# One fused decoder kernel on Trainium2: attention issued by upper and lower heads in turn

## The chip, the cores and the metric

The kernel runs on one core of a Trainium2 chip. The metric is the device time of one execution in microseconds. The engines are TensorE (PE; its weight loads are PEld), VectorE (DVE), ScalarE (ACT), GpSimd (POOL) and SyncE (SP), which here issues DMAs. Each has its own instruction stream, takes it in order, and waits on semaphores where it needs another engine's result.

## What is computed

256 tokens of width 1024 in fp32 go through: an even layer (sliding-window attention with 8 heads beside a state space mixer), a feed-forward net, an odd layer (stick-breaking attention with 16 heads), a second feed-forward net, a third one, the mix stage (spatial gating beside dilated-window attention with 8 heads), cross attention, a last feed-forward net and a norm. The heads are 64 wide in the three attentions that matter here. The parts of the reference that the change touches, cut:

```python
# even layer
scores = einsum('bnqhgd,bnkhd->bnhgqk', qb, kb) * d ** -0.5     # banded mask
m = maximum(scores.max(-1), sink); p = exp(scores - m)
o = einsum(..., p / (p.sum(-1) + exp(sink - m)), vb)
out = y * sigmoid(y @ w_glu + b_glu)                            # y: the SSM's gelu'd output
mixed = concatenate([o_attn, o_ssm], -1) @ even_w_out
# odd layer: A[t,s] = beta_ts * prod_{s<j<t}(1 - beta_tj), s < t
z = einsum('bhqd,bhkd->bhqk', q, k) * scale
log_keep = where(mask, log_sigmoid(-z), 0)
log_survive = cumsum(log_keep, reverse=True) - log_keep
w = where(mask, exp(log_sigmoid(z) + log_survive), 0);  o = einsum(w, v)
# mix stage
y_a = chunked_spatial_gating(z_sgu);  y_b = dilated attention(q, k, v)
y = concatenate([rmsnorm(y_a), rmsnorm(y_b)], -1);  x = x + y @ w_out
```

## The kernel before

Activations stay in SBUF as two token tiles of 128. Weights stream in by DMA in tiles of 128x1024 (`raw`); ACT casts each to its upper part (L293, `whi`) and DVE subtracts for the lower part (L295, `wlo`). Where full precision is wanted, a product is three TensorE products (L320, L321, L322): upper by upper, lower by upper, upper by lower. These are the "GEMM products" below.

A list scheduler sets the order on every engine from the order in which the program is written, so what the text issues in a row may be interleaved with other work. The coarse order of the three stages is set by strings: `EVEN`, `ODD` and `MIX`, whose two-letter items name pieces (`10` is step 0 of the attention of token tile 1; `g0` in `MIX` is the gating of tile 0; `K0` to `K3` are projections of the memory for the later cross attention, work that depends on nothing in the stage).

PSUM has eight banks of 128 partitions by 512 fp32 in three pools: `mm` (2), `tr` (2) and `acc` (4).

A head is 64 wide, so two heads lie one above the other in the 128 partitions: the lower half (0 to 63) and the upper half (64 to 127). A score product has 64 rows of contraction and uses half the rows of the array. A value product has 64 output rows and uses half the columns.

`attention()` serves the even stage (t0 and t1) and the mix stage. Its `step(g)` takes `per` heads of one half: one score bank (`mm`), the mask added by a product with the identity (L587), the scores (L591), maximum, exponential (L605), normalisation (L612), four transposes (L401), one copy out of PSUM (L619), and the value products (L625) into the bank `po`. There are 2 steps for t0 and 4 for t1.

In the odd stage `scores(b, half)` takes four heads of one half and three blocks (lower keys by lower queries, lower by upper, upper by upper), each in its own `acc` bank: mask (L1188), scores (L1191), DVE minimum (L1194), ACT Exp (L1195). `weights` follows with Ln (L1206), DVE maximum (L1207), the cast `sph` and the remainder `spl` (L1210, L1211), products with triangular and all-one matrices (L1218) and Exp (L1221, `w0` and `w1`). `values` (L1234, L1236) writes two `tr` banks. `before(q)` writes the outputs of the state space mixer (L1094). `ssm_gate` transposes them (L401 out of `s0`), splits them (DVE copy L1114, ACT cast L1115, DVE L1116) and multiplies by the gate's weights.

In the mix stage `normed` (L1309 to L1314) is run for both halves of the output, `oa` (gating) and `ob` (attention), each for two token tiles: ACT Square, POOL addition, PE column sums (L419), DVE mean (L423), POOL power (L424), DVE diagonal (L426), PE broadcast (L429), ACT copy (L431), DVE scaling (L1314), ACT cast (L396), DVE remainder (L397). Then `w_out` takes `oa` first.

Of the kernel before, what the change touches and what calls it, by code (L numbers as in the profile page):

```python
# [16 lines left out]
P = 128  # L17
# [220 lines left out]
class Kernel:  # L238
# [331 lines left out]
    def attention(self, pool, t, qt, kt, kblock, v, vcol, bias, nsink):  # L570
# [12 lines left out]
        def step(g):  # L583
            sc = self.ps("mm")
            scv = sc.rearrange("p (h k) -> p h k", h=per)
            for m, bt in enumerate(bias):
                nc.tensor.matmul(sc, self.ident_r, bt, start=(m == 0), stop=False)  # L587
            for i in range(per):
                half, qb = divmod(g * per + i, 4)
                r = slice(half * 64, half * 64 + 64)  # L590
                nc.tensor.matmul(scv[:, i, :], qt[r, qb, t * P:(t + 1) * P],  # L591
                                 kt[r, kblock(qb), 0:keys], start=False, stop=(i == per - 1))
            hs = slice(g * per, (g + 1) * per)
# [8 lines left out]
            pr = self.t(pool, [P, per, keys], "prob", bufs=4)  # L602
            for i in range(per):
                h = g * per + i
                nc.scalar.activation(pr[:, i, :], scv[:, i, :], AF.Exp, bias=mneg[:, h:h + 1],  # L605
                                     scale=SCALE, accum_out=den[:, h:h + 1])
# [11 lines left out]
            pt = self.t(pool, [P, 4, P], "prob", bufs=4)  # L618
            nc.scalar.copy(pt, tp.rearrange("p (c n) -> p c n", c=4))  # L619
            for i in range(per):  # L620
                half, qb = divmod(g * per + i, 4)
                r = slice(half * 64, half * 64 + 64)
                h = 2 * qb + half
                for b in range(nk):
                    nc.tensor.matmul(po[r, qb * P:(qb + 1) * P], v[b][:, vcol(h):vcol(h) + 64],  # L625
                                     pt[:, i * nk + b, :], start=(b == 0), stop=(b == nk - 1))

        return [lambda g=g: step(g) for g in range(8 // per)], po.rearrange("p (b n) -> p b n", b=4)


# [430 lines left out]
    def ssm_out(self, ep, uu, S):  # L1061
# [26 lines left out]
        def before(q):  # L1088
            hs = S["hs"]
            for gl in range(4 * q, 4 * q + 4):  # L1090
                bank, cols = at(gl)
                r = (gl % 2) * 64
                for ri in range(2):
                    nc.tensor.matmul(yb[bank][r:r + 64, cols], hs[ri][:, gl, :], gts[q][:, ri, gl % 4],  # L1094
                                     start=False, stop=(ri == 1), skip_group_check=True)
# [7 lines left out]
    def ssm_gate(self, ep, gy):  # L1103
# [16 lines left out]
        for pr in range(2):  # L1120
# [6 lines left out]
            for b in range(2):  # L1127
                o = 2 * pr + b
                sg = self.t(ep, [P, 256], "prob", bufs=4)
                nc.scalar.activation(sg, ps[:, b * 256:(b + 1) * 256], AF.Sigmoid,  # L1130
                                     bias=self.prm[:, PR_BGLU + o:PR_BGLU + o + 1])
                y = self.t(ep, [P, 256], "prob", bufs=4)
# [24 lines left out]
    def odd(self):  # L1157
# [18 lines left out]
        blocks = ((lo_, lo_), (lo_, hi_), (hi_, hi_))  # L1176

        parts = {}

        def scores(b, half):  # L1180

            r = slice(half * 64, half * 64 + 64)
            zs, raw = [], []
            for n, (s, t) in enumerate(blocks):
                z = self.ps("acc")
                zv = z.rearrange("p (h t) -> p h t", h=4)
                if n != 1:
                    nc.tensor.matmul(zv, self.ident_r, stk.unsqueeze(1).to_broadcast([P, 4, P]),  # L1188
                                     start=True, stop=False)
                for i in range(4):  # L1190
                    nc.tensor.matmul(zv[:, i, :], kt[r, b * 4 + i, s], qt[r, b * 4 + i, t],  # L1191
                                     start=(n == 1 and i == 0), stop=(i == 3))
                sp = self.t(op, [P, 512], "sp", bufs=3)
                nc.vector.tensor_scalar(sp, z, 40.0, None, ALU.min)  # L1194
                e = nc.scalar.activation(sp, sp, AF.Exp).ins  # L1195
                zs.append(z)
                raw.append(sp)
            parts[b, half] = zs, raw, e

        def weights(b, half):  # L1200
            zs, raw, e = parts[b, half]
            sps = []
            for z, sp in zip(zs, raw):

                with self.tc.issue_after(e):
                    nc.scalar.activation(sp, sp, AF.Ln, bias=1.0)  # L1206
                nc.vector.tensor_tensor(sp, sp, z, ALU.max)  # L1207
                sh = self.t(op, [P, 512], "sph", F32R, bufs=3)
                sl = self.t(op, [P, 512], "spl", F32R, bufs=3)
                nc.scalar.copy(sh, sp)  # L1210
                nc.vector.tensor_tensor(sl, sp, sh.bitcast(F32), ALU.subtract)  # L1211
                sps.append((sh, sl))
            w0 = self.t(op, [P, 4, 256], "w0", bufs=2)
            w1 = self.t(op, [P, 4, P], "w1", bufs=2)
# [344 lines left out]
```

## Time and profile before

| | us |
|---|---|
| time, median of 3 runs | 1247.03 |
| lowest and highest | 1245.78, 1249.15 |
| profiled execution, own time | 1243.83 |
| its span in the trace | 1242.1 |
| PE busy | 1211.7 (98%) |
| DVE busy | 868.8 (70%) |
| ACT busy | 676.6 (54%) |
| POOL busy | 211.2 (17%) |

The span is what the trace covers; the own time is 1.73 us longer. Approximate stages in the span: even layer 0 to 165, feed-forward to 343, odd layer 343 to 475, feed-forward nets to 840, mix 840 to 975, cross attention to 1030, the last feed-forward net and norm to the end. A matmul's busy time includes its passage through the array, so consecutive ones overlap in the records; the distance between two starts is their pace.

### The profile page before, as it was taken

To read this page: it belongs to the slowest core of one execution; us is meant where nothing else is said; L and a number is where in the kernel's file an instruction comes from. 1 tells how busy PE (TensorE), PEld (TensorE's weight loads), DVE (VectorE), ACT (ScalarE), POOL (GpSimd) and SP (SyncE) were. 2 spreads that over 40 slices of the span, in tenths; PEclk is the share of its full clock that TensorE was granted. 3 is DMA by queue.
4 is the path that set the end of the run, shared out by engine and by line. 5 is a ranking of instruction groups with operands and counts; after the bars stand their busy time and mean duration, and the time that the engine had idled before them with its cause. 6 is when DMAs were issued, how large, how long until landed. Compare 5 with 4: busy or idle time off the path is not lost.

```text
span 1242.1 us, 19044 instructions
## 1 busy us (share of the span) xinstructions
PE 1211.7 (98%) x7686; PEld 1072.7 (86%) x7686; DVE 868.8 (70%) x1191; ACT 676.6 (54%) x1052; POOL 211.2 (17%) x177
## 2 busy tenths in 40 slices
PE   6889999999999999999999999999999999999997
PEld 6777998888899879888888888888889999888886
DVE  8978588777665647877766867766866656777752
ACT  6543566565446755655545655545664545655542
POOL 7665021110010002101001110002201101111000
PEclk9978999999999999999999999999999999999998
DMA  6541355555553325455654545646633434555551
GB/s 208 172 158 53 139 172 194 180 201 203 180 197 110 131 68 204 170 187 186 216 191 174 196 177 198 204 174 212 209 131 103 155 118 139 190 183 201 204 200 38
DMA packets 36776, 208.86 MB, mean 168 GB/s; under 512 B 3920, under 2 KB 9808, under 8 KB 12752
## 3 DMA queue, kind: packets, MB, share of 16 engines
q1 hardware_dynamic: 35824, 205.48, 47.7%
q0 software_dynamic: 576, 1.64, 0.5%
q8 instruction: 60, 0.98, 0.3%
q10 hardware_dynamic: 288, 0.52, 0.1%
q14 instruction: 28, 0.23, 0.1%
HBM read 205.57 MB, written 2.06 MB: 167 GB/s over the span
## 4 chain that ended last, share of the span: by engine, by line
PE 92%; DVE 5%; DMA 1%; issue 1%; ACT 1%; POOL 0%; DVEq 0%; ACTq 0%
PE acc L367 26%; PE acc L366 13%; PE mm L367 13%; PE mm L366 7%; PE mm L320 4%; PE mm L322 4%; PE mm L321 4%; PE acc L322 4%; PE acc L321 4%; PE acc L320 4%; PE mm L591 1%; PE tr L401 1%; PE acc L1191 1%; DVE wlo L295 1%; PE acc L625 1%; DVE a L454 1%
## 5 line engine op out<-in xcount | busy, mean ns | idle before, releaser
L295 DVE TENSOR_TENSOR wlo<-raw,whi 128x1024 fp32r<-128x1024 f32 (+1 forms) x378 | 472.0, 1251 | 225.1 <-ACT whi L293 223.6
L293 ACT CAST whi<-raw 128x1024 fp32r<-128x1024 f32 (+1 forms) x378 | 392.4, 1043 | 280.8 <-DMA raw<-in_wts 111.2
L367 PE MATMUL acc<-h,whi 128*128 128x512 f32 x704 | 247.8, 397 | 0.0
L367 PE MATMUL mm<-a,whi 128*128 128x512 f32 x704 | 247.0, 392 | 0.0
L367 PE MATMUL acc<-a,whi 128*128 128x512 f32 x704 | 246.0, 392 | 0.0
L366 PE MATMUL acc<-h,wlo 128*128 128x256 f32 x704 | 196.9, 281 | 0.0
L366 PE MATMUL mm<-a,wlo 128*128 128x256 f32 x704 | 196.6, 281 | 0.0
L366 PE MATMUL acc<-a,wlo 128*128 128x256 f32 x704 | 196.3, 280 | 0.0
L367 PEld LDWEIGHTS acc<-h,whi 128*128 128x128 f32 x704 | 131.9, 188 | 32.0
L367 PEld LDWEIGHTS mm<-a,whi 128*128 128x128 f32 x704 | 131.5, 187 | 28.5
L367 PEld LDWEIGHTS acc<-a,whi 128*128 128x128 f32 x704 | 130.9, 187 | 28.2
L366 PEld LDWEIGHTS acc<-a,wlo 128*128 128x128 f32 x704 | 133.0, 189 | 1.0
L366 PEld LDWEIGHTS acc<-h,wlo 128*128 128x128 f32 x704 | 132.9, 189 | 0.3
L366 PEld LDWEIGHTS mm<-a,wlo 128*128 128x128 f32 x704 | 132.6, 189 | 0.2
L546 POOL TENSOR_TENSOR sg<-sg,rb 128x512 f32<-128x512 f32 x44 | 58.2, 1326 | 388.8 <-ACT sg L545 379.2
L463 POOL TENSOR_TENSOR ssq<-ssq,sq 128x512 f32<-128x512 f32 x26 | 39.7, 1528 | 416.7 <-ACT sq L461 253.2
L320 PE MATMUL mm<-a,whi 128*128 128x256 f32 x224 | 66.4, 298 | 6.7 <-ACT whi L293 6.7
L321 PE MATMUL acc<-a,whi 128*128 128x256 f32 x240 | 67.4, 284 | 0.0
L322 PE MATMUL acc<-a,wlo 128*128 128x256 f32 x240 | 67.1, 285 | 0.0
L322 PE MATMUL mm<-a,wlo 128*128 128x256 f32 x224 | 66.1, 296 | 0.8 <-DVE wlo L295 0.7
L320 PE MATMUL acc<-a,whi 128*128 128x256 f32 x240 | 66.0, 286 | 0.0
L321 PE MATMUL mm<-a,whi 128*128 128x256 f32 x224 | 65.8, 295 | 0.0
(371 smaller groups left out, 1951.5 us busy)
## 6 DMA issues: line engine op xcount, KB each, us to landing
raw<-in_wts SPq DMA_DIRECT2D x187, 1024.0 KB, 4.9
raw<-in_mem SPq DMA_DIRECT2D x4, 512.0 KB, 5.6
eb<-lag SPq DMA_DIRECT2D x4, 512.0 KB, 4.8
x<-in_x SPq DMA_DIRECT2D x4, 256.0 KB, 5.3
raw<-in_wts SPq DMA_DIRECT2D x4, 256.0 KB, 5.6
sprm<-in_prm SPq DMA_DIRECT2D x1, 512.0 KB, 9.1
ud<-s SPq DMA_DIRECT2D x1, 512.0 KB, 2.6
uu<-ud SPq DMA_DIRECT2D x8, 64.0 KB, 5.3
```

Of the source, the lines that this page charges most:

```text
L293: nc.scalar.copy(hi[:, c:c + n], src)
L295: nc.vector.tensor_tensor(lo[:, c:c + n], src, hi[:, c:c + n].bitcast(F32), ALU.subtract)
L320: mm(out, a[0], b[0], start=start, stop=False, skip_group_check=True)
L321: mm(out, a[0], b[1], start=False, stop=False, skip_group_check=True)
L322: mm(out, a[1], b[0], start=False, stop=stop, skip_group_check=True)
L366: mm(out[:, 0, :], w[1], x[:, 0], start=first, stop=False, skip_group_check=True)
L367: mm(out, w[0], x, start=False, stop=last, skip_group_check=True)
L401: self.nc.tensor.transpose(out, in_, self.ident[:k, :k])
L454: lo = nc.vector.scalar_tensor_tensor(lo, x[:, b, :], g, hi.bitcast(F32), ALU.mult, ALU.subtract).ins
L463: nc.gpsimd.tensor_tensor(ssq, ssq, q, ALU.add)
L546: nc.gpsimd.tensor_tensor(sg, sg, rb2, ALU.mult)
L591: nc.tensor.matmul(scv[:, i, :], qt[r, qb, t * P:(t + 1) * P], kt[r, kblock(qb), 0:keys], start=False, stop=(i == per - 1))
```

## The change

`attention`'s step now holds both halves: two score banks, both masked, then score products lower, upper, lower, upper; a softmax for each half; one tile `probt` for both; value products lower, upper in turn. t0 has 1 step instead of 2 and t1 has 2 instead of 4, so the strings lose items. In the mix stage the scores use `acc` banks and the gating `mm`.

In the odd stage a step is a pair of head blocks with both halves. It needs four `acc` banks instead of three (two full, two half): lower keys against all 256 queries, and upper keys against upper queries. There are four minima and four maxima instead of three each, four Exps at the end instead of three, and as many Exp, Ln, casts and remainders as before. `values(b)` then needs only its own step. `before(q)` writes the two halves of the partitions in turn.

The diff, cut:

```diff
-EVEN = "p0 i0 N x1 W0 t0 p1 i1 h0 W1 h1 i2 m0 m1 00 x0 10 i3 W2 s0 W3 11 12 01 x2 m2 g0 13 g1 g2 m3 x3 g3"
+EVEN = "p0 i0 N x1 W0 t0 p1 i1 h0 W1 h1 i2 m0 m1 x0 10 i3 W2 s0 00 W3 11 x2 m2 g0 g1 g2 m3 x3 g3"
-MIX = "x N v w y r0 r1 u0 10 u1 00 K0 11 g0 01 12 g1 13 K1 K2 K3"
+MIX = "x N v w y r0 r1 u0 10 u1 00 K0 11 g0 g1 K1 K2 K3"
...
-            sc = self.ps("mm")
...
+            scs = [self.ps(tag) for _ in range(2)]
+            for sc in scs:
+                for m, bt in enumerate(bias):
+                    nc.tensor.matmul(sc, self.ident_r, bt, start=(m == 0), stop=False)
+            for i in range(per):
+                qb = g * per + i
+                for half in range(2):
+                    r = slice(half * 64, half * 64 + 64)
+                    nc.tensor.matmul(scv[half][:, i, :], qt[r, qb, t * P:(t + 1) * P],
+                                     kt[r, kblock(qb), 0:keys], start=False, stop=(i == per - 1))
+            pt = self.t(pool, [P, 2, 4, P], "probt")
+            for half in range(2):
+                softmax(half, g, scv[half], pt[:, half])
+            for i in range(per):
+                for b in range(nk):
+                    for half in range(2):
+                        nc.tensor.matmul(po[r, qb * P:(qb + 1) * P], v[b][:, c:c + 64],
+                                         pt[:, half, i * nk + b, :], start=(b == 0), stop=(b == nk - 1))
...
-        def scores(b, half):
+        def scores(b, j):
+            z0 = [self.ps("acc").rearrange("p (h t) -> p h t", h=2) for _ in range(2)]
+            z1 = [self.ps("acc")[:, :256].rearrange("p (h t) -> p h t", h=2) for _ in range(2)]
+            for z, s, t in ((z0, lo_, slice(0, 256)), (z1, hi_, hi_)):
+                for i in range(2):
+                    for h, r in enumerate(halves):
+                        nc.tensor.matmul(z[h][:, i, :], kt[r, blk, s], qt[r, blk, t], ...)
...
         def gating(t):
-            ps = self.ps("acc")
+            ps = self.ps("mm")
```

The scheduler turns this into new orders. Three places follow; names end in the number of the tile.

PE in the last step of the odd stage. `acc_725` to `acc_729` are the score banks, `acc_754` (before) is a bank of the stage's output projection, `mm_733` (after) a value projection, `sph` and `spl` what `weights` delivers, `tr_752` and `tr_753` value banks. Before:

```order
L320 MATMUL acc_754_4452<-o_620_3554,whi_739_4364 128x256
L321 MATMUL acc_754_4452<-o_620_3554,whi_739_4364 128x256
L322 MATMUL acc_754_4452<-o_620_3554,wlo_740_4365 128x256
L1234 MATMUL tr_752_4430<-w0_709_4193,v0_616_3550 64x256
L1234 MATMUL tr_753_4441<-w0_709_4193,v0_616_3550 64x256
L1218 MATMUL acc_725_4300<-sph_743_4400,trih_613_3544 128x512
L1218 MATMUL acc_725_4300<-spl_744_4401,trih_613_3544 128x512
L320 MATMUL acc_754_4452<-o_620_3554,whi_741_4368 128x256
L321 MATMUL acc_754_4452<-o_620_3554,whi_741_4368 128x256
L1218 MATMUL acc_727_4309<-sph_745_4406,trih_613_3544 128x512
L1218 MATMUL acc_729_4317<-sph_747_4412,trih_613_3544 128x512
```

After, between the last scores and the end of this piece:

```order
L321 MATMUL mm_733_4342<-wlo_722_4264,a_597_3493 128x512
L322 MATMUL mm_733_4342<-whi_721_4263,a_597_3493 128x512
L1255 MATMUL tr_753_4451<-w0_709_4203,v0_613_3547 64x256 x2
L1258 MATMUL tr_753_4451<-w1_710_4204,v1_614_3548 64x128 x2
L1255 MATMUL tr_753_4451<-w0_709_4203,v0_613_3547 64x256 x2
L1258 MATMUL tr_753_4451<-w1_710_4204,v1_614_3548 64x128 x2
L1237 MATMUL acc_725_4315<-sph_744_4420,trih_610_3541 128x512
L1237 MATMUL acc_726_4316<-sph_746_4424,trih_610_3541 128x512
L1242 MATMUL acc_727_4317<-sph_748_4428,trih_610_3541 128x256
L1242 MATMUL acc_728_4318<-sph_748_4428,trih_610_3541 128x256
L1237 MATMUL acc_725_4315<-spl_745_4421,trih_610_3541 128x512
```

Before, products of the output projection stand among these rows; after, the step's own four banks are all of the `acc` pool, and only 12 products of the value projection and one set of value products stand between the last scores and the first product with `sph_744`.

PE around the output projection of the even stage. `s0_75` holds the state space mixer's output, `et` the attention's, `acc_243` the projection, `mm_264` the gate. Before:

```order
L625 MATMUL acc_182_996<-prob_239_1354,qkv0_67_382 64x128
L625 MATMUL acc_182_996<-prob_239_1354,qkv1_68_383 64x128
L401 MATMUL tr_259_1528<-ident_6_80,s0_75_395 128x128 x4
L401 MATMUL tr_260_1536<-ident_6_80,s0_75_395 128x128 x4
L320 MATMUL acc_243_1406<-et_230_1304,whi_197_1077 128x256
L320 MATMUL acc_244_1407<-et_230_1304,whi_197_1077 128x256
L320 MATMUL acc_245_1408<-et_230_1304,whi_197_1077 128x256
L321 MATMUL acc_243_1406<-et_231_1305,whi_197_1077 128x256
```

After:

```order
L321 MATMUL acc_243_1406<-et_218_1216,whi_222_1225 128x256
L322 MATMUL acc_243_1406<-et_217_1215,wlo_223_1226 128x256
L401 MATMUL tr_256_1525<-ident_6_80,s0_75_395 128x128 x4
L401 MATMUL tr_257_1533<-ident_6_80,s0_75_395 128x128 x4
L320 MATMUL mm_264_1552<-a_255_1524,whi_245_1409 128x256
L320 MATMUL mm_269_1589<-a_255_1524,whi_245_1409 128x256
L321 MATMUL mm_264_1552<-a_255_1524,whi_245_1409 128x256
```

The transposes of `s0` stood ahead of the 96 products of the projection and now stand behind them, directly ahead of the gate's products, which take what is made from them (`a_255`).

PE and ACT at the end of the mix stage. `mm_1611` is a product of `K3`; `tr_1589` (before), `tr_1571`, `tr_1579` and `tr_1587` (after) are the banks of `normed`; `acc_1612` and `acc_1610` are of `w_out`; `a_1433` (before) and `a_1434` (after) are `oa`. PE before:

```order
L322 MATMUL mm_1611_9244<-m1_1450_8341,wlo_1598_9121 128x256
L320 MATMUL mm_1611_9244<-m1_1450_8341,whi_1597_9120 128x256
L419 MATMUL tr_1589_9096<-ones_1_73,sq_1588_9093 128x1 x2
L321 MATMUL mm_1611_9244<-m1_1450_8341,whi_1597_9120 128x256
L322 MATMUL mm_1611_9244<-m1_1450_8341,wlo_1598_9121 128x256
```

PE after:

```order
L633 MATMUL acc_1523_8697<-probt_1565_9010,vt1_1431_8280 64x128 x2
L419 MATMUL tr_1571_9048<-ones_1_73,sq_1570_9045 128x1 x2
L419 MATMUL tr_1579_9081<-ones_1_73,sq_1578_9078 128x1 x2
L429 MATMUL tr_1571_9048<-diag_1573_9054,ones_1_73 128x128
L419 MATMUL tr_1587_9114<-ones_1_73,sq_1586_9111 128x1 x2
L429 MATMUL tr_1579_9081<-diag_1581_9087,ones_1_73 128x128
L429 MATMUL tr_1587_9114<-diag_1589_9120,ones_1_73 128x128
L320 MATMUL acc_1610_9312<-a_1434_8283,whi_1599_9194 128x256
```

The norms of before lie among `K3`'s products; after, three norms stand in a row between the last values and `w_out`. ACT before (`sq` the Square, `ya` the gating, `acc_1512` an attention output):

```order
L619 COPY prob_1542_8843<-tr_1541_8838 128x512
L605 ACTIVATE prob_1551_8917,den_1519_8673<-mm_1550_8910,mneg_1520_8674 128x256 x2
L1309 ACTIVATE sq_1556_8945<-ya_1555_8942 128x512
L619 COPY prob_1553_8927<-tr_1552_8922 128x512
L605 ACTIVATE prob_1563_8975,den_1509_8647<-mm_1562_8966,mneg_1510_8648 128x128 x4
L431 COPY rn_1560_8957<-tr_1557_8948 128x128
L619 COPY prob_1565_8987<-tr_1564_8982 128x512
L605 ACTIVATE prob_1573_9021,den_1519_8673<-mm_1572_9014,mneg_1520_8674 128x256 x2
L396 CAST a_1433_8262<-yn_1561_8959 128x4x128
L1309 ACTIVATE sq_1566_8993<-acc_1512_8650 128x512
L1309 ACTIVATE sq_1578_9049<-ya_1577_9046 128x512
```

ACT after:

```order
L431 COPY rn_1554_8930<-tr_1551_8921 128x128
L396 CAST a_1435_8284<-yn_1555_8932 128x4x128
L293 CAST whi_1615_9318<-raw_1614_9316 128x1024
L1331 ACTIVATE sq_1570_9045<-acc_1523_8697 128x512
L1331 ACTIVATE sq_1578_9078<-ya_1577_9075 128x512
L1331 ACTIVATE sq_1586_9111<-ya_1585_9108 128x512
L431 COPY rn_1574_9057<-tr_1571_9048 128x128
L431 COPY rn_1582_9090<-tr_1579_9081 128x128
L396 CAST a_1435_8284<-yn_1575_9059 128x4x128
L396 CAST a_1434_8283<-yn_1583_9092 128x4x128
```

Before, the Squares of `ya` lie among the exponentials of the attention; after, both come behind the Square of the last attention output, `acc_1523`.

## Rows read from the trace of the kernel before

**Rows 1.** Page, busy time of each engine, and chain that ended last by engine.

```profile
PE 1211.7 (98%) x7686; PEld 1072.7 (86%) x7686; DVE 868.8 (70%) x1191; ACT 676.6 (54%) x1052; POOL 211.2 (17%) x177
...
PE 92%; DVE 5%; DMA 1%; issue 1%; ACT 1%; POOL 0%; DVEq 0%; ACTq 0%
```

**Rows 2.** Windows, odd and mix: window, length, PE busy, granted clock, DMA share, GB/s.

```profile
343.00:475.00 132.00, 132.00 (x892) 1.00 0.38 131
840.00:975.00 135.00, 133.56 (x880) 1.00 0.47 158
```

**Rows 3.** Timeline of PE, odd scores of one half: start, us, instruction, count.

```profile
374.91 1.16 PE L1191 MATMUL acc<-qt,kt 64*128 64x128 f32 x8
375.99 0.50 PE L1188 MATMUL acc<-stkh,identr 128*128 128x512 f32 x1
```

**Rows 4.** Timeline of PE, mix: values of one half, then gating with halves alternating.

```profile
923.96 0.98 PE L625 MATMUL acc<-prob,vt 128*64 128x128 f32 x7
...
924.83 1.96 PE L1357 MATMUL acc<-ws,sv 128*64 128x128 f32 x29
```

**Rows 5.** Groups by line and shape, mix: count, busy, mean ns, idle before.

```profile
L625 PE MATMUL acc<-prob,vt 128*64 128x128 f32 x48 | 6.5, 279 | 1.1 <-ACT prob L619 1.1
L591 PE MATMUL mm<-kt,qt 64*128 64x256 f32 x16 | 4.8, 408 | 0.0
...
L591 PE MATMUL mm<-kt,qt 64*128 64x128 f32 x16 | 2.6, 291 | 0.0
```

**Rows 6.** Groups by line and shape, odd stage: the scores.

```profile
L1191 PE MATMUL acc<-qt,kt 64*128 64x128 f32 x96 | 13.9, 285 | 0.0
```

**Rows 7.** Timeline and windows of PE, even stage: idle time, and granted clock behind it.

```profile
62.81 0.58 PE L322 MATMUL acc<-whi,a 128*128 128x256 f32 x1 [2.96 <-DVE a L454]
...
83.57 1.10 PE L401 MATMUL tr<-ident,qkv 128*128 128x128 f32 x6 [2.09 <-DVE lsb L1020]
...
64.00:66.00 2.00, 2.00 (x12) 0.50 0.01 5
...
68.00:70.00 2.00, 2.00 (x19) 1.00 0.98 381
...
84.00:101.00 17.00, 16.99 (x123) 0.52 0.23 69
```

**Rows 8.** Timeline of ACT, last odd step: Exp, table load, Ln.

```profile
443.17 0.63 ACT L1195 ACTIVATE sp<-sp 128x512 f32<-128x512 f32 x1 [0.88 <-DVE sp L1194]
443.82 1.28 ACT L1206 ACT_TABLE_LOAD   x1
445.11 1.68 ACT L1206 ACTIVATE sp<-sp 128x512 f32<-128x512 f32 x3
```

**Rows 9.** Timeline, even stage: splits of the transposed output, start of the gate's products.

```profile
137.91 1.18 ACT L1115 CAST a<-tr 128x512 fp32r<-128x512 f32 x2 [1.35 <-DVE s L1114]
...
148.29 0.28 PE L320 MATMUL mm<-a,whi 128*128 128x256 f32 x1
...
148.41 0.28 PE L321 MATMUL mm<-a,whi 128*128 128x256 f32 x1
...
149.71 1.05 ACT L293 CAST whi<-raw 128x1024 fp32r<-128x1024 f32 x1 [0.64 <-DMA raw<-in_wts]
```

**Rows 10.** Timeline, end of the mix stage: the links of the last norm.

```profile
953.53 0.60 ACT L1309 ACTIVATE sq<-acc 128x512 f32<-128x512 f32 x1 [1.09 <-PE acc L625]
...
954.21 0.73 POOL L1310 TENSOR_TENSOR sq<-sq 128x256 f32<-128x256 f32 x1 [8.27 <-ACT sq L1309]
...
957.30 0.50 PE L419 MATMUL tr<-ones,sq 128*128 128x1 f32 x4
...
958.09 0.55 POOL L424 TENSOR_TENSOR rs<-rs,nhalf 128x1 f32<-128x1 f32 x1 [3.14 <-DVE rs L423]
...
962.11 1.13 DVE L1314 SCALAR_TENSOR_TENSOR yn<-acc,prm,rn 128x128 f32<-128x128 f32 x4 [0.98 <-ACT rn L431]
...
963.27 0.62 ACT L396 CAST a<-yn 128x512 fp32r<-128x512 f32 x1 [1.19 <-DVE yn L1314]
```

More of the change, by code (lines that the diff above doesn't have):

```diff
@@ L567, in ffn, with attention @@
         stack.close()
-    def attention(self, pool, t, qt, kt, kblock, v, vcol, bias, nsink):
+    def attention(self, pool, t, qt, kt, kblock, v, vcol, bias, nsink, tag="mm"):
         nc = self.nc
@@ L581, in attention, with softmax @@
         po = self.ps("acc")
-        def step(g):
-            sc = self.ps("mm")
[L585 to L593, printed above, removed]
+        def softmax(half, g, scv, pt):
+            hs = slice(half * 4 + g * per, half * 4 + (g + 1) * per)
             nc.vector.tensor_reduce(mx[:, hs], scv, axis=AX.X, op=ALU.max)
@@ L601, in step @@
                 nc.vector.tensor_tensor(es, mneg[:, hs], nsink[:, hs], ALU.subtract)
-            pr = self.t(pool, [P, per, keys], "prob", bufs=4)
+            pr = self.t(pool, [P, per, keys], "prob", bufs=2)
             for i in range(per):
-                h = g * per + i
+                h = hs.start + i
                 nc.scalar.activation(pr[:, i, :], scv[:, i, :], AF.Exp, bias=mneg[:, h:h + 1],
@@ L1089, in before @@
             hs = S["hs"]
[L1090 to L1092 removed]
+            for g2 in range(4 * q, 4 * q + 4, 2):
                 for ri in range(2):
[L1094 to L1095 removed]
+                    for gl in (g2, g2 + 1):
+                        bank, cols = at(gl)
+                        r = (gl % 2) * 64
+                        nc.tensor.matmul(yb[bank][r:r + 64, cols], hs[ri][:, gl, :], gts[q][:, ri, gl % 4],
+                                         start=False, stop=(ri == 1), skip_group_check=True)
             if q % 2 == 1:
@@ L1175, in odd @@
         lo_, hi_ = slice(0, P), slice(P, 256)
-        blocks = ((lo_, lo_), (lo_, hi_), (hi_, hi_))
+        halves = [slice(h * 64, h * 64 + 64) for h in range(2)]
         parts = {}
-        def scores(b, half):
[L1182 to L1198, printed above, removed]
@@ L1200, in weights @@
-        def weights(b, half):
-            zs, raw, e = parts[b, half]
-            sps = []
[L1203 to L1211, printed above, removed]
-                sps.append((sh, sl))
-            w0 = self.t(op, [P, 4, 256], "w0", bufs=2)
-            w1 = self.t(op, [P, 4, P], "w1", bufs=2)
-            for n, terms in enumerate((((tri, 0),), ((tri, 1), (one, 2)), ((tri, 2),))):
-                flat = [(m, x) for m, src in terms for x in sps[src]]
-                for j, (m, x) in enumerate(flat):
-                    nc.tensor.matmul(zs[n], m, x, start=False, stop=(j == len(flat) - 1),
-                                     skip_group_check=True)
-                dst = w1 if n == 2 else w0[:, :, n * P:(n + 1) * P]
-                nc.scalar.activation(dst, zs[n].rearrange("p (h t) -> p h t", h=4), AF.Exp)
-            parts[b, half] = w0, w1
```

80 lines of the change are left out of this document (61 added, 19 removed).

## The prediction

> **What bounds the kernel now.** I read the busy times and the chain that ended last first, then the same by stage, then PE's waits. PE is busy 1211.7 of 1242.1 us and holds 92% of the chain [rows 1]. In the odd stage it is busy 132.00 of 132.00 us, in the mix stage 133.56 of 135.00, at full clock in both [rows 2]. So a microsecond of PE work taken out of these stages is a microsecond of time, if nothing else comes late in its place. In the even stage PE does wait, up to 2.96 us at a time [rows 7]. The other engines have room, but room on average: at one place each engine is a link of a chain, and there its latency counts.
>
> **What the change removes: PE time in half-filled tiles.** One half's values start 0.98 - 0.27 = 0.71 us over six distances, 0.12 us per product of 128 columns (0.27 being roughly one product alone, an estimate from the mean of 0.279 [rows 5]); the gating, which already alternates halves of the columns, starts 28 distances in 1.96 - 0.28 us, 0.06 us each [rows 4]. Alternating column halves therefore halves the pace. For row halves no row of before shows two next to each other: eight scores of one half take 375.99 - 374.91 = 1.08 us, 0.135 each with the change of tile shape at the end [rows 3]. So the gain for rows lies between 0 and 0.06 us per product; I take 0.06, by the nearest row, the columns.
>
> By the Trainium skill, TensorE: Matmul & The Clock Gate, Part 3, four row tiles at once came out 3.07 times as fast as one after the other, so pairs overlap, if not fully; by that proportion (an estimate) each gain below would be about a tenth to a quarter smaller, some 2 to 3 us in all. The column pace of rows 4 agrees; no row here shows the row case.
>
> Now the count, in products of 128 columns (a score against 256 keys counts two). The odd scores are 96 [rows 6], the mix scores 16 x 2 + 16 = 48, the mix values 48 [rows 5]. In the order of after I counted how many stand directly beside one of the other half and did not before. Scores: 64 in the odd stage (its last step issues its first bank pair half after half), 44 in mix, 16 in even (where two of three steps are issued half after half): 124 x 0.06 = 7.4 us. Values and state outputs: 44 odd (before, a third already stood in mixed runs), 36 mix, 36 even, less 4 that the state outputs lose: 112 x 0.06 = 6.7 us. The state outputs in `before(q)` count nothing: the scheduler had mixed them already. Small-tile runs become eight fewer (3 odd, 4 mix, 1 even). The run of eight scores takes 1.08 us where eight paces of 0.12 make 0.96 [rows 3]; with as much again at its other end one run costs some 0.25 us: 2.0 us. Together -16.1 us; the odd stage has -7.2, mix -5.8, even -3.1.
>
> What it adds on DVE and ACT (four small instructions on DVE, six on ACT, shorter ones for longer) I cost at nothing: both engines are idle a third of the time and PE's GEMM products cover them, except at three places.
>
> **What it moves: three holes in PE's queue.** At each I take the orders of after and put rows' durations on the links, T being the end of the last PE work ahead.
>
> *Odd stage, last step.* The four banks of the step fill `acc`, so the output projection, which covered this chain before, must wait. After the last score PE has 12 products of 512 columns at 0.24 (twice the 0.12 us from 148.29 to 148.41 for 256 columns [rows 9]) and a set of values, about 3.9 us. The chain: minimum and last Exp to T + 1.1, table load 1.28, three Ln in 1.68 [rows 8], but ACT's order puts two weight casts of 1.05 [rows 9] and one copy out of PSUM (some 0.6) among them, then the cast of `sph` (0.6, as [rows 10] has it): T + 7.3. Hole 3.4. Then the products wait for later `spl` and for the first of the final Exps behind another table load: 1.3 more. Hole 4.7; if the casts came sooner, 2.5.
>
> *Even stage, gate.* The transposes of `s0` stand directly ahead of the gate. ACT's order has a weight cast ahead of the two casts; before, its data came only at 149.71, 1.4 us after the gate began [rows 9]. So: cast to T + 2.7, two casts of 1.18 together to 3.9, remainder on DVE to about 5.2 for L321. PE has 1.1 us of transposes and two products: hole 4.0. With the data earlier 1.8.
>
> *Mix stage, end.* `w_out` takes `oa` first, and both its norms come behind the Square of the last attention output. One norm is 0.60 + 0.73 + 0.5 + 0.55 + 1.13 + 0.62 = 4.1 us in its long links [rows 10], 5.2 with the short ones (an estimate). Three in a row share ACT, POOL and DVE: three Squares (the third must wait until the first's buffer is read, after L419), then power after power, then L1314 three times at 1.13. Step by step I get the last cast of `oa` at T + 10.5, with 2.6 us of L419 and L429 on PE meanwhile: hole 8.0. If the three overlapped ideally, third Square to T + 1.8 and then one norm: T + 6.8, hole 4.2.
>
> Sum of the holes: 16.7 us, between 8.5 and 18. Before, these places had none: the work stood among GEMM products.
>
> **The clock.** After 2.96 us of idle PE the granted clock was 0.50, and at 64 to 66 us it still was; after the idles that end with 2.09 us at 83.57 it was 0.52 for 17 us [rows 7], PE busy with small tiles throughout. So a hole like these costs more than itself: some 4 us at half speed give away about 2 us. Three holes: 6.2 us, between 0 (the hole at the end of mix is broken by L419 and L429) and 8.
>
> By the same page, in its section on HAM oscillation, every wait of this kind throttles TensorE anew and the cost is paid each time; rows 7 agree, with two idles and two falls.
>
> **The sum.** -16.1 + 16.7 + 6.2 = +6.8. The profiled execution took 1243.83 us; that gives 1250.6. The median of the runs is 3.2 us above that execution, so the forecast for the median is 1254.
>
> **Rivals.** (1) *Row halves do not overlap*: the change then does only half of what it says. For it: no row shows it. Against: columns do it. 7.4 us are lost: 1261. (2) *The holes are at their short ends*, because ACT and DVE have the weight casts behind them when the links come: 8.5 us instead of 16.7, the clock's cost the same: 1246, no change. For it: ACT is busy 54%. Against: the orders are fixed and the casts stand among the links. (3) *The clock gives back*, faster than before. The stretch 84 to 101 at 0.52 holds scores and values of one half at a time; under full-width products the clock was back by 70 [rows 7]. If filled tiles bring it back about as soon, up to 17 x 0.48 = 8.2 us are won there, and if the holes, cut up by small products, do not lower it again, 6.2 are not lost: 1247 - 16.1 + 16.7 - 8.2 = 1239.4. It decides when clock losses come out over 3 us below before's instead of 6 above. Against: the idles that lead into that stretch stand ahead of every changed instruction.
>
> The Trainium skill's TensorEngine Tiling (Array Packing), Key Properties, says that a change of tiling mode drains the array while a change of tile does not; by it alternating halves is free and only the runs count, as I have it. Its Gotcha 1 wants different banks for different row tiles; the change gives each half its own, which speaks against rival 1.
>
> **Chances.** Forecast 0.50 (1249 to 1260), rival 1 0.14, rival 2 0.22 (1241 to 1249), rival 3 0.14. The range that leaves out 2 in 10 goes from 1240 to 1262. Within 0.3% (1243.3 to 1250.8), about what a measurement of this kernel can tell from no change: 0.24, most of rival 2 and the near end of the forecast. Faster: 0.16. Slower: 0.60.
>
> **What would show it.** Odd scores and values: starts 0.06 apart, and the odd stage's PE work about 7 us shorter; starts 0.12 apart mean rival 1. PE waits of 3 to 5 us at the first product with `sph` of the last odd step (L1237, on ACT) and at the gate's first products (L320 or L321, on ACT or DVE), and about 8 us between the last values of mix and `w_out` (L429 and L320). If the mix hole is under 5 us, the step with three norms in a row was wrong. Clock 0.5 for some 4 us behind each hole; no fall means 6 us less.

## The result, and the profile after

The changed kernel takes 1256.72 us (median of 4 runs, 1255.95 to 1257.4), the kernel before beside it on the same chip 1246.40 (1243.48 to 1249.15). The ratio is 1.0083, with an interval from 1.0059 to 1.0107: slower, by 10.3 us. The profiled execution of after took 1257.4 us with a span of 1255.4, 13.3 us longer than the span of before.

The page of after, busy time of each engine and the chain that ended last, answers to [rows 1]:

```profile
PE 1201.8 (96%) x7678; PEld 1064.1 (85%) x7678; DVE 869.0 (69%) x1199; ACT 676.8 (54%) x1056; POOL 209.7 (17%) x177
...
PE 84%; DVE 6%; DMA 4%; ACT 3%; issue 2%; POOL 1%; SPq 0%; DVEq 0%; ACTq 0%; POOLq 0%
```

PE is busy 9.9 us less than before, and yet the kernel is 13.3 us longer: PE's idle time grew by 23.2 us. Both sides of the prediction, less work and new holes, are in these two numbers, but not all of the idle time costs something: 3.3 us of the growth lie at 32 us in the even stage, ahead of every changed instruction, and by the wait that ends at 62.45 us after has lost nothing (in before it ends at 62.81). By stage, the windows of before: even, odd, mix with cross attention (window, length, PE busy, granted clock, DMA share, GB/s):

```profile
0.00:165.58 165.58, 144.73 (x1145) 0.92 0.45 149
...
350.70:478.81 128.11, 128.11 (x880) 1.00 0.38 132
...
849.80:1045.07 195.27, 193.83 (x1383) 1.00 0.44 152
```

and the same stretches of after, each cut at the start of the same product (the round stage limits of before, given ahead of the prediction, lie up to 15 us off):

```profile
0.00:172.49 172.49, 141.57 (x1145) 0.88 0.43 143
...
357.60:485.84 128.24, 122.92 (x871) 0.99 0.39 132
...
856.84:1058.04 201.20, 192.02 (x1384) 0.97 0.43 147
```

The feed-forward nets between them, which the change does not touch, agree to 0.01 us (185.12 and 185.11, 370.99 and 371.00). The even stage lost 6.9 us, the odd stage is unchanged (+0.1: 5.2 us less PE work, 5.3 us more idle), the mix stage with cross attention lost 5.9.

The new line numbers, for the rows that follow: in `attention` L617 is the mask (L587 before), L622 the scores (L591), L597 the Exp (L605), L633 the values (L625); in the odd stage L1196 and L1199 are the masks, L1204 the scores, L1228 the cast `sph`, L1237 to L1242 the triangular products, L1243 the Exp of `w`, L1255 and L1258 the values; L1124 and L1125 are the split at the gate, L1332 the addition of the norm.

**Pace.** The trace shows each fp32 score or value product as two records (the 8 score products of an odd step are 16); counts of scores and values here, as in the prediction, are of records. Scores and values of after in the timeline (mix scores and values, then one odd step's scores):

```profile
914.96 1.13 PE L622 MATMUL acc<-kt,qt 64*128 64x256 f32 x8
916.03 0.39 PE L322 MATMUL mm<-a,wlo 128*128 128x256 f32 x1
...
943.43 1.09 PE L633 MATMUL acc<-probt,vt 128*64 128x128 f32 x14
...
382.06 1.58 PE L1204 MATMUL acc<-qt,kt 64*128 64x256 f32 x16
383.57 0.39 PE L320 MATMUL mm<-a,whi 128*128 128x256 f32 x1
```

In before four mix scores of one half stand in the same 1.06 us between starts:

```profile
903.78 1.13 PE L591 MATMUL mm<-kt,qt 64*128 64x256 f32 x4
904.84 0.39 PE L320 MATMUL mm<-a,whi 128*128 128x256 f32 x1
```

Eight in the time of four: row halves overlap in full. An odd step's scores are 24 units of 128 columns in 1.51 us, 0.063 each, where [rows 3] had 0.135.

**The holes.** The timeline of PE in after at the gate, in the odd stage, and at the end of mix (start, us, instruction, in brackets the idle time before it and its releaser):

```profile
151.03 0.61 PE L320 MATMUL mm<-a,whi 128*128 128x256 f32 x2 [2.70 <-ACT a L1124]
152.75 0.58 PE L321 MATMUL mm<-a,whi 128*128 128x256 f32 x1 [1.11 <-DVE a L1125]
...
401.01 0.38 PE L1196 MATMUL acc<-stkh,identr 128*128 128x256 f32 x1 [1.65 <-ACT w L1243]
...
430.49 1.08 PE L1255 MATMUL tr<-w,v 128*64 128x256 f32 x8 [0.64 <-ACT v L1181]
...
455.42 0.69 PE L1258 MATMUL tr<-w,v 128*64 128x128 f32 x4 [2.69 <-ACT v L1181]
...
957.34 1.09 PE L633 MATMUL acc<-probt,vt 128*64 128x128 f32 x14
960.50 1.29 PE L419 MATMUL tr<-ones,sq 128*128 128x1 f32 x8 [2.08 <-POOL sq L1332]
962.84 0.49 PE L429 MATMUL tr<-diag,ones 128*128 128x128 f32 x2 [1.05 <-DVE diag L426]
963.77 0.98 PE L419 MATMUL tr<-ones,sq 128*128 128x1 f32 x4 [0.45 <-ACT rn L431]
...
967.12 0.80 PE L429 MATMUL tr<-diag,ones 128*128 128x128 f32 x2 [1.73 <-DVE diag L426]
970.15 1.23 PE L320 MATMUL acc<-a,whi 128*128 128x256 f32 x4 [2.24 <-ACT a L396]
```

The gate's hole is 3.81 us. The end of mix has five waits, 7.55 us. In the odd stage, whose four steps start their scores near 382, 401, 423 and 446 us, the idle times are 1.65 in the second step, 0.64 in the third, 2.69 and 0.33 in the last: 5.31 together, of which 3.02 in the last step.

**The clock.** Windows of after behind the gate's hole, the odd hole and in the mix hole, every engine:

```profile
154.00:158.00 4.00, 4.00 (x20) 4.00 (x20) 0.00 (x0) 0.00 (x0) 0.00 (x0) 0.50 0.00 0
158.00:160.00 2.00, 2.00 (x18) 2.00 (x17) 0.96 (x2) 1.25 (x3) 0.00 (x0) 0.97 0.00 0
...
456.00:460.00 4.00, 4.00 (x22) 2.77 (x18) 3.82 (x6) 3.78 (x7) 0.00 (x0) 0.69 0.75 262
...
964.00:968.00 4.00, 2.19 (x8) 1.60 (x8) 3.22 (x12) 1.40 (x3) 0.55 (x1) 0.50 0.00 0
```

The granted clock is 0.50 (1.2 GHz) behind the gate's hole until 158, with PE's queue full of GEMM products; from 152 on some 3.0 us are lost. Behind the odd hole it is 1.2 to 1.7 us. At the end of mix the 18 products from 970.15 to 973.93 start about 0.21 us apart instead of 0.12, which loses 1.8 us:

```profile
971.18 0.41 PE L321 MATMUL acc<-a,whi 128*128 128x256 f32 x1
971.39 0.41 PE L322 MATMUL acc<-a,wlo 128*128 128x256 f32 x1
```

L419 and L429 take 2.0 us more in this stage than in before; how much of that is the clock and how much that they stand alone between waits is not separated.

### The profile page after: what moved, and what is told of

It is laid out like the page before. It is cut to its first block, busy times and chain, and to the rows that moved or that the text cites. A ratio compares the mean times of both kernels' runs of the same rounds, so it can differ in the third digit from the quotient of the medians.

```text
span 1255.4 us, 19045 instructions
## 1 busy us (share of the span) xinstructions
PE 1201.8 (96%) x7678; PEld 1064.1 (85%) x7678; DVE 869.0 (69%) x1199; ACT 676.8 (54%) x1056; POOL 209.7 (17%) x177
## 4 chain that ended last, share of the span: by engine, by line
PE 84%; DVE 6%; DMA 4%; ACT 3%; issue 2%; POOL 1%; SPq 0%; DVEq 0%; ACTq 0%; POOLq 0%
PE acc L367 26%; PE acc L366 13%; PE mm L367 13%; PE mm L366 7%; PE acc L320 3%; PE acc L321 3%; PE acc L322 3%; PE mm L321 2%; PE mm L320 2%; DMA raw<-in_wts 2%; PE mm L322 2%; DVE wlo L295 2%; PE tr L401 1%; DMA raw<-in_mem 1%; ACT whi L293 1%
## 5 line engine op out<-in xcount | busy, mean ns | idle before, releaser
L320 PE MATMUL mm<-a,whi 128*128 128x256 f32 x224 | 66.0, 297 | 10.1 <-ACT whi L293 6.3
L320 PE MATMUL acc<-a,whi 128*128 128x256 f32 x240 | 66.1, 290 | 2.2 <-ACT a L396 2.2
L322 PE MATMUL acc<-a,wlo 128*128 128x256 f32 x240 | 68.1, 288 | 0.0
L322 PE MATMUL mm<-a,wlo 128*128 128x256 f32 x224 | 66.0, 296 | 1.3 <-DVE wlo L295 1.3
```

Source lines behind the costliest of these rows:

```text
L320: mm(out, a[0], b[0], start=start, stop=False, skip_group_check=True)
L322: mm(out, a[1], b[0], start=False, stop=stop, skip_group_check=True)
```

## The experiments

Each kernel computes the whole reference. "Stage" below means the stretches cut as above, in that kernel's profiled execution. The diffs are cut.

**Undo one part.** Three kernels, each with one stage's attention as before and the rest as in after.

e1, `attention` of before in the mix stage:

```diff
-MIX = "x N v w y r0 r1 u0 10 u1 00 K0 11 g0 g1 K1 K2 K3"
+MIX = "x N v w y r0 r1 u0 10 u1 00 K0 11 g0 01 12 g1 13 K1 K2 K3"
```

> The mix stage alone goes back to one half per step, with its order string and banks of before; even and odd stay changed. Theory A (each stage pays for its own holes): between the last product of the feed-forward net ahead of mix and the first of the one behind cross attention the changed kernel takes 201.2 us, before 195.3; so 5.9 us come back, 1250.8 us, and PE's waits at L419, L429 and L320 at the end of mix vanish. Rival B (time lost in one stage is given back or lost again in a later one): no change, 1256 to 1257.

1252.34 us, 1.0055 times before (1.0035 to 1.0076). The mix stage with cross attention takes 195.43 us, 5.8 less than after and about what before has (195.27). The window where after has its hole (columns as above):

```profile
950.00:980.00 30.00, 30.00 (x251) 29.70 (x250) 17.28 (x29) 11.54 (x15) 1.30 (x3) 1.00 0.38 131
```

e2, the even stage as before (its string, `attention` and `ssm_gate`, `before(q)`):

```diff
-EVEN = "p0 i0 N x1 W0 t0 p1 i1 h0 W1 h1 i2 m0 m1 x0 10 i3 W2 s0 00 W3 11 x2 m2 g0 g1 g2 m3 x3 g3"
+EVEN = "p0 i0 N x1 W0 t0 p1 i1 h0 W1 h1 i2 m0 m1 00 x0 10 i3 W2 s0 W3 11 12 01 x2 m2 g0 13 g1 g2 m3 x3 g3"
```

> The even stage alone (attention, state outputs, order string) goes back. Theory A: the first feed-forward net began at 172.5 us in the changed kernel and at 165.6 before; 6.9 us come back, 1249.8 us. Rival B: a good part of those 6.9 us lies ahead of the first changed instruction (the profile shows waits of 2.2 us at L429 and 0.45 us at L401 before 80 us, where the orders are the same) and stays: 1253 us or more.

1253.95 us, 1.0069 (1.0054 to 1.0084). The even stage takes 166.40 us, 6.1 less than after, without a wait at the gate. But the odd stage, which is that of after, took 131.77 in this execution, not 128.24 (see e6).

e3, the odd stage as before:

```diff
-            z0 = [self.ps("acc").rearrange("p (h t) -> p h t", h=2) for _ in range(2)]
-            z1 = [self.ps("acc")[:, :256].rearrange("p (h t) -> p h t", h=2) for _ in range(2)]
...
+        blocks = ((lo_, lo_), (lo_, hi_), (hi_, hi_))
```

> The odd stage alone goes back. Theory A: gains of about 7 us there are eaten by 5.3 us of waits and 1.7 us of clock; net 0.1 us, so 1256.6 us, and the odd stage between the feed-forward nets stays at 128 us while its four waits vanish. Rival B: pairing row halves brings nothing in the odd stage, so that the holes are a net loss: about 1252 us.

1257.57 us, 1.0091 (1.0074 to 1.0108), the time of after; the odd stage takes 128.28. So the odd stage's gain and its holes cancel, and the loss sits in the even and the mix stage. By the ratios e1 and e2 give back 3.5 and 1.7 us of the 10.3, less than the 5.8 and 6.1 of their stages; both intervals overlap that of after, so the medians alone show neither, and the reading rests on the stages. In the profiled e2 the odd stage took 3.5 of it; whether that holds for the other runs the medians can't tell.

**Mend one hole.** The gating issued ahead of the mix attention (e4), and the gate's transposes, copies, casts and remainders issued ahead of the 96 products of the even projection (e6), both with everything else as in after.

```diff
-MIX = "x N v w y r0 r1 u0 10 u1 00 K0 11 g0 g1 K1 K2 K3"
+MIX = "x N v w y r0 r1 u0 10 u1 g0 g1 00 K0 11 K1 K2 K3"
```

> The changed kernel with one edit: in the order string of the mix stage the two gatings stand ahead of the last steps of the attention (g0 g1 before 00, K0, 11), so that their norms are done long before the output projection, which takes them first. Theory A (the end of mix is a hole of 7.5 us plus 2 us of slower clock, made by three norms in a row): 9 us come back, about 1247.5 us, no wait over 1 us at the end of mix. Rival B (the hole is the last attention step's own chain, and only moves): at most 3 us, 1253.5 us or more.

1250.47 us, 1.0037 (1.0013 to 1.006): by the ratios 5.7 us of the 10.3 are back from two items moved in one string, less than the 9 of theory A and more than the 3 of rival B. No profile of it is read; e7 has the same edit.

```diff
+        split = self.ssm_split(ep, y)
         acc = self.proj_out([oa], "even_w_out", 0, (0, 2))
-        osm = self.ssm_gate(ep, y)
+        osm = self.ssm_gate(ep, *split)
```

> The changed kernel with one edit: in the even stage the transposes of the state outputs and their splits are written ahead of the output projection, so that the scheduler sets them among its 96 products, as before. Theory A: the waits of 2.7 and 1.1 us at the gate's first products go, and the 6 us at half clock behind them (3 us lost): 6 to 7 us come back, 1250 us. Rival B (the half clock comes from elsewhere and the wait moves ahead of the projection): at most 3 us, 1254 us or more.

1253.4 us, 1.0042 (1.0023 to 1.0061): 5.1 us back by the ratios, with intervals that overlap slightly. The even stage takes 165.13 us instead of 172.49, without the wait for the gate's split; before has 165.58. Its odd stage, unchanged against after, took 131.82. Windows of PE in e6 behind a wait of 1.29 us at L1202 (the mask, L1196 of after):

```profile
394.00:398.00 4.00, 4.00 (x21) 0.70 0.00 0
398.00:402.00 4.00, 4.00 (x20) 0.50 0.00 0
402.00:406.00 4.00, 4.00 (x34) 0.95 0.71 262
```

and in after, where the same place waits 1.65 us:

```profile
401.00:404.00 3.00, 2.99 (x18) 1.00 0.01 5
404.00:408.00 4.00, 4.00 (x36) 1.00 0.00 0
```

So the changed odd stage has two levels, near 128.2 (after, e1, e7) and near 131.7 (e2, e5, e6), according to whether the clock falls behind that wait.

e7, both edits together:

> Both mends on the changed kernel: gatings early in the order string of the mix stage, state outputs split early in the even stage. Theory A: the end of mix has no wait over 1 us and mix with cross attention takes 192 to 193 us instead of 201 to 203; the even stage 165 to 167 instead of 172; 1241 us, faster than before. Rival B (holes only move): over 1247 us.

1244.03 us, 0.9984 (0.9955 to 1.0012): both holes mended, the change is worth nothing measurable, where 1241 was expected. The even stage takes 164.72, odd 128.44, mix and cross 195.72, not the 192 to 193 of theory A but what before has. At the end of mix one wait is left:

```profile
965.46 0.36 PE L320 MATMUL acc<-a,whi 128*128 128x256 f32 x1 [0.90 <-DVE yn L1342]
```

**The odd stage.** e8 is e7's mix stage with the even stage of before and with the three-bank odd steps of before, whose `values` alternate the halves:

```diff
-                for half in range(2):
-                    r = slice(half * 64, half * 64 + 64)
-                    w0, w1 = parts[b, half]
-                    for i in range(2):
...
+                for i in range(2):
...
+                    for half in range(2):
+                        r = slice(half * 64, half * 64 + 64)
```

> Only what pays by theory A: the mix stage as changed with its gatings early; the even stage as before; the odd stage as before with three banks per step, but with the value products of the two halves in turn. Expected: even stage 166 us, odd 125.5 to 126.5 (128.1 before; 44 value products save 0.06 us each, and there is no four-bank wait), mix with cross attention 190 to 192 (195.3 before); 1239 us. Rival B (values in the odd stage already overlapped by the scheduler's mixing, mix gains eaten by the last step's chain): 1244 us or more.

1242.36 us, 0.9961 (0.9943 to 0.9978). The odd stage takes 124.49 us with PE busy 124.18: 3.6 less than in before, with 0.31 of idle. The four-bank step wins more PE work (122.92 busy) and gives all of it back in waits. The rest of the expectation was missed: the even stage took 167.80 us, and the mix stage with cross attention 198.06 where 190 to 192 was expected. The same instructions took 195.72 in e7, so the length of a stage in a single execution is good to some 2 us only.

e11 is the kernel before with that edit of `values` alone:

> The kernel before with one part of the change alone: in the odd stage the value products of the two halves in turn, scores and weights as before. Theory A: odd stage 124.5 us instead of 128.1, the rest as before: 1243 us. Rival B (the odd stage of the run without four banks gained by chance): 1246.5 us.

1243.59 us, 0.9968 (0.995 to 0.9985), odd stage 124.49: the same 3.6 us from the values alone. (Its profiled execution is 6.6 us over its median; the second pair of feed-forward nets has four waits for `wlo`, 4.0 us, that no other profile has. Only the odd stage is read.)

e9 takes the odd `v` out of PSUM on DVE instead of ACT, with the rest as in after:

```diff
-            self.gemm_tok(ops, name, 0, base + n * 512, lambda t, ps: nc.scalar.activation(
-                dst[t][:, n * 512:(n + 1) * 512], ps, AF.Copy, scale=rs[t]))
+            self.gemm_tok(ops, name, 0, base + n * 512, lambda t, ps: nc.vector.tensor_scalar(
+                dst[t][:, n * 512:(n + 1) * 512], ps, rs[t], None, ALU.mult))
```

> The changed kernel, but the odd stage's values leave PSUM through DVE instead of ACT, so that their copy no longer stands behind the last step's Exp, Ln and weight casts in ACT's queue. Theory A (ACT's chain from the scores to sph sets the hole of the last step): the 2.7 us wait at L1258 for v goes, and a wait of 1.5 to 2.5 us appears at L1237 for sph; the odd stage stays at 127 to 128 us (131 to 132 in executions in which the clock falls twice), in all 1256 us. Rival B (the late link is the copy of v alone): both go, odd stage 125 us, 1253 us.

1258.8 us, 1.0091 (1.0065 to 1.0117). Neither theory came: the wait stays, 0.4 us shorter, and changes its releaser. PE and DVE in the timeline of e9:

```profile
451.39 0.44 PE L1258 MATMUL tr<-w,v 128*64 128x128 f32 x4 [2.30 <-DVE v L1181]
...
449.39 1.29 DVE L1223 TENSOR_TENSOR sp<-sp,acc 128x512 f32<-128x512 f32 x2 [2.70 <-ACT sp L1221]
450.59 0.75 DVE L1181 TENSOR_SCALAR v<-mm,rs 128x512 f32<-128x512 f32 x1
```

and ACT in the timeline of after:

```profile
450.89 1.28 ACT L1221 ACT_TABLE_LOAD   x1
452.18 1.15 ACT L1221 ACTIVATE sp<-sp 128x512 f32<-128x512 f32 x2
...
454.17 0.62 ACT L1221 ACTIVATE sp<-sp 128x512 f32<-128x512 f32 x1
454.70 0.67 ACT L1181 ACTIVATE v<-mm,rs 128x512 f32<-128x512 f32 x1
```

In after the copy of `v` stands on ACT behind the table load, three Lns and a weight cast; in e9 it stands on DVE behind two maxima (L1223), which wait 2.70 us for the same Lns. Either way the last step's chain lies ahead of the copy. So the wait does not hang on the engine of the copy; that its place in the order makes it is what the two timelines suggest, but no run moved the copy ahead. The odd stage takes 130.02 us here: the clock held behind the first wait (1.72 us at L1196) and was 0.50 from 453 to 463 us, longer than in after.

**Alternating or adjacent.** e5 issues the scores of both halves in one run, but first all of the lower half, then all of the upper, in all three stages:

```diff
-                for i in range(2):
-                    blk = 4 * b + 2 * j + i
-                    for h, r in enumerate(halves):
+                for h, r in enumerate(halves):
+                    for i in range(2):
+                        blk = 4 * b + 2 * j + i
```

> The changed kernel, but the score products of a step are issued half after half instead of in turn, in all three stages; banks, steps and values stay. Theory A (two halves of the rows run at once, 0.06 us saved per product of 128 columns): some 3.8 us more PE work in the odd stage, 2.6 in mix, 1.0 in even, so 7 us more, 1264 us, less what of it falls into waits that are there anyway; two full score banks take 0.12 us per product of 128 columns instead of 0.07. Rival B (alternating rows brings nothing, the gain is the columns'): 1257 us as without the edit.

1263.53 us, 1.0126 (1.0092 to 1.0161). Its timeline, one odd step and one mix step:

```profile
387.11 1.68 PE L1204 MATMUL acc<-qt,kt 64*128 64x256 f32 x16
388.72 0.39 PE L320 MATMUL mm<-a,whi 128*128 128x256 f32 x1
...
924.62 1.14 PE L622 MATMUL acc<-kt,qt 64*128 64x256 f32 x8
925.69 0.39 PE L322 MATMUL mm<-a,wlo 128*128 128x256 f32 x1
```

1.61 us between starts instead of 1.51, and 1.07 as in after: the scores overlap nearly as well where two products (four records) of one half stand ahead of two of the other. In the step for t0 of the mix stage four products (eight records) of one half stand ahead of four of the other, and there the overlap is lost in part, after first, then e5:

```profile
928.63 1.16 PE L622 MATMUL acc<-kt,qt 64*128 64x128 f32 x14
...
935.55 1.49 PE L622 MATMUL acc<-kt,qt 64*128 64x128 f32 x14
```

In e5 the first four records start alone, 0.11 to 0.21 us apart, and the other half joins at the fifth. Over the mix stage the edit costs the scores 0.34 us. The time is that of theory A, but not for its reason: most of the 6.8 us over after (5.4 by the ratios) stands elsewhere, in the even stage (177.54) and the odd stage (131.55), mix being 201.76; e3, whose even stage is that of after, has 175.48, so the even stage spreads by itself, and how much of e5's time belongs to its edit stays open.

**All mended.** e10 has e7's two edits, the odd stage of e8, and the mix projection `y` in `acc` banks:

```diff
-XACC = ('w', 'x')
+XACC = ('w', 'x', 'y')
```

> Even stage changed with the early split; odd stage as before with value products in turn; mix stage changed with early gatings, and one more edit: the projection y (the values) writes acc banks, so that the masks of the scores cannot take two of them early and the next projection does not wait for ACT to empty mm (the wait of 1.1 to 1.6 us for vt at L320). Theory A: even 165, odd 124.5, mix with cross attention 192 to 193 (195.7 with early gatings alone): 1239 us. Rival B (that wait is covered elsewhere, mix stays at 195 to 196): 1242 us.

1236.18 us (1232.53 to 1242.4, 6 runs), 0.991 (0.9884 to 0.9936): faster than both kernels. Its windows, even, odd, and mix with cross (PE):

```profile
0.00:164.29 164.29, 139.57 (x1144) 0.90 0.45 150
349.40:473.96 124.56, 124.25 (x879) 1.00 0.39 136
845.63:1037.09 191.46, 189.39 (x1383) 1.00 0.45 155
```

The edit of `y` was not run with the mix stage of before, so how much of the 191.46 us (195.27 in before, 195.72 in e7) needs the changed attention stays open. Nor does any run vary one more part of the change, the buffers of `prob`, 2 instead of 4.

## Why the prediction was right, and where its terms were off

The forecast was 1254.0 us in a range from 1240 to 1262; measured were 1256.72. The likeliest case came, slower, with the mechanism as told: less PE work, three holes, and the clock behind them. That the odd stage's term fits is in part luck. Against the medians the sum +6.8 stands beside +10.3, against the two profiled executions beside +13.6. Stage by stage, with the clock's 6.2 us divided evenly, as 2.1 for each hole:

| us | predicted | measured |
|---|---|---|
| odd: gain, holes, clock | -7.2 + 4.7 + 2.1 = -0.4 | -6.4 to -6.9, +5.3, +1.2 to 1.7: +0.1 |
| even | -3.1 + 4.0 + 2.1 = +3.0 | +6.9 (five changed ones, e5's among them, 169.5 to 177.5; four as in before 165.3 to 167.8) |
| mix and cross: gain, holes, clock | -5.8 + 8.0 + 2.1 = +4.3 | -5.6, +7.7, +3.8: +5.9 |

**Rival 1 fell, as it was given little.** Row halves overlap in full (1.07 us for eight, 1.06 for four), and 0.06 us per product was right for rows. The prediction's estimate from the Trainium skill (TensorE: Matmul & The Clock Gate, Part 3, four row tiles 3.07 times as fast) had pairs fall short of that; here they do not, and no run has four row tiles.

**The gain in the odd stage was right.** PE's busy time there fell by 5.2 us; with the 1.2 to 1.7 us that the half clock lost the gain is 6.4 to 6.9, predicted 7.2.

**The gain in mix was right, the clock's cost there was not.** Distances from start to start, idle time left out, summed over the stretch of mix and cross: scores 6.79 to 3.64 us, values 5.92 to 4.16, together -4.9, where 80 products by 0.06 gave -4.8. Masks and gating give 0.7 more, in all -5.6 for the -5.8 of the sum. Yet PE's busy time in this stretch fell by 1.8 us only, and the reason lies at the end of the stage. The GEMM products (L320 to L322), the same number of them, went from 150.7 to 152.5 us, which is the 1.8 us of the 18 products at half clock, and L419 and L429 took 2.0 us more. The prediction had 2.1 us for both. The waits come to 7.7 us: 7.55 at the end and 1.56 in the middle, less 1.44 that before had.

In e7, whose clock is 1.00 in that stage, the GEMM products took 152.7 us for another reason: 41 of those with 256 columns start over 0.15 us after the one ahead, against 28 in before and 29 in after outside the 18, and this makes 1.6 us of what e7 lacks to its expectation. What makes them late was not tried.

**The gate's hole was right**, 3.81 us for 4.0, at the products named; its clock cost 3.0 for 2.1. e6, e7 and e10, with the split early, do not have this wait, and their even stage takes 164.3 to 165.1.

**The even stage's other loss was missed.** In after the timeline of PE shows, before the projection:

```profile
94.74 0.50 PE L617 MATMUL mm<-swah,identr 128*128 128x512 f32 x1 [2.32 <-ACT prob L597]
...
102.46 1.12 PE L401 MATMUL tr<-ident,prob 128*128 128x128 f32 x4 [0.68 <-ACT probt L610]
```

A step now holds both `mm` banks, so the next step's mask must wait for this step's Exps; the 0.68 us are a wait for a `tr` bank, which the copy L610 empties. The prediction counted four banks of the odd stage but not two of two here. In e2, with the old step, the wait at the same place is 0.20 us. Around it the clock, windows of PE in after:

```profile
90.00:92.00 2.00, 2.00 (x59) 1.00 0.01 2
...
108.00:110.00 2.00, 2.00 (x17) 0.50 0.00 0
110.00:112.00 2.00, 2.00 (x16) 0.92 0.00 0
```

Rival 3 was half true: with filled tiles the clock was back at 90 us, where before it stayed near 0.5 until 101 [rows 7]. That holds for every profile read: back by 88 to 93 us in all eight with the changed even stage, by 100 to 103 in the four with the old one. Behind the wait at 94.74 it was lost again until 110, and in each of the eight it fell once more behind a wait at this line. From the idle at L401 behind `lsb` to the projection's end, where the gain of 3.1 should have shown, after is only about 1.0 us ahead. A further 0.9 us of the 6.9 lies before 84.51, ahead of the changed instructions (2.25 us idle there at 84.51, in before 2.09 at 83.57).

**The odd hole was right in sum by luck, not in place.** 4.7 was predicted for the last step, the first of it at L1237 on `sph`. The last step's waits are 2.69 and 0.33, 3.02 together, at the values L1258 and L1255, the larger of them ahead of L1237 in PE's order, since the `v` it needs comes through the same ACT queue as the Lns and casts. Another 0.64 us stand in the third step, also for `v`, and 1.65 us in the second, at L1196: the next step's four banks wait for the final Exps of the one before. The prediction looked at the last step alone; e8 and e11, with three banks, have neither.

**The mix hole was right**, 7.55 us for 8.0, and its reason too: with the gating's norms moved ahead only 0.90 us of it is left in e7, and e4, with that edit alone, gets 5.7 us back by the ratios. Missed were two smaller waits in the middle, 1.09 us for `vt` (at L320) and 0.47 for `qt` (at L401), because the attention's masks take two `acc` banks early and `y` is left to two `mm` banks; with `y` in `acc` (e10) the one for `vt` is gone. The masks cannot be its only reason: e11, with the mix stage of before, waits 1.05 us at the same place.

**Rival 2**, the holes at their short ends, fell at the gate (3.81, short end 1.8) and in mix (7.55, short end 4.2). In the last odd step 3.02 us lie nearer its 2.5 than the 4.7 of the sum. The error of the sum is the missed waits (3.0 in even, 1.65 and 0.64 in odd, 1.6 in mix) with the clock behind the first of them, and 1.7 us more for the slow clock at the end of mix; in the odd stage a last step 1.7 us shorter than predicted made up for most of the missed waits there.

## What to carry to other kernels

Filling both halves of the array was worth its 0.06 us per product of 128 columns here only where the step that holds both halves left a bank and some independent work: count, per pool, the banks that one step holds and the ones that the next step's first instruction needs. When the steps become fewer and longer, look at what used to lie between them (here a gate's split, and three norms) and issue that work earlier; moving it took the change from 10.3 us slower to no difference, and taking the value products in turn within the old steps, with `y` in other banks, to 11.3 us faster than before (e10 against the 1247.49 of its own chip). Try the part that needs no more banks first: it alone was worth 3.6 us in its stage.

## What was not expected of the hardware

Row halves need not alternate strictly. Eight scores, four of the lower half and then four of the upper, took 1.07 us between starts, as did eight in turn, against 1.06 for four of one half; sixteen, in groups of four, took 1.61 against 1.51. With eight of one half ahead of eight of the other the first four ran alone, and fourteen records took 1.49 us instead of 1.16. This goes by the order in which e5 issues the products; the two halves stood in one run and in different banks each time.

The same wait does not always cost the same: behind 1.29 us of idle the granted clock fell to 0.50 in e6, behind 1.65 us at the same place in after it stayed at 1.00. It fell in e2 (1.78 us) and e5 (1.48) too, and stayed in e1 (1.48), e7 (1.85) and e9 (1.72), so the length of the wait alone does not decide it. That is a difference of 3.5 us in the odd stage, from one execution to another, which no sum made from one profile holds.
